# Fox q and k token-major, conditioning columns in another order and at other rates, five load buffers in turn

## The chip, the cores and the metric

The kernel runs on one core of a Trainium2 chip. The metric is the time of one execution in microseconds as the device reports it, the median of several runs. TensorE (PE) multiplies matrices, VectorE (DVE) and ScalarE (ACT) work on vectors, GpSimd (POOL) issues some of the transfers here and SyncE (SP) issues most of them. A weight load of PE is shown as PEld.

## What is computed

A trunk of two layers on 256 tokens of width 2048, all in float32. Both layers have the same frame; the mixer of the first is an mLSTM, that of the second is Forgetting Attention (Fox), and the change touches the second.

```
for layer in range(DEPTH):
    mod = cs @ ada_w[layer] + ada_b[layer]           # cs = silu(c); 6 vectors of 2048 a layer
    sh1, sc1, g1, sh2, sc2, g2 = split(mod, 6)
    h = rms_norm(x, norm_mix_w[layer]) * (1 + sc1) + sh1
    x = x + g1 * mixer(h)
    h = rms_norm(x, norm_ffn_w[layer]) * (1 + sc2) + sh2
    x = x + g2 * swiglu(h, ffn_w_gate_up[layer], ffn_w_down[layer])
return rms_norm(x, final_norm_w)

def fox_mixer(h, w_in, b_f, w_out):                  # 16 heads of 128
    q, k, v, fl = split(h @ w_in, [2048, 4096, 6144])
    cum = cumsum(log_sigmoid(fl + b_f))
    o = softmax(q @ k.T * 128 ** -0.5 + cum[t] - cum[s], causal) @ v
    return o @ w_out
```

The six vectors of `mod` are the conditioning columns: 2 layers of 96 columns of 128 values, each the product of a 128 x 2048 tile of `ada_w` with `cs`.

## The kernel before

**Matrix products.** A float32 weight is split into a high part `hi` (rounded to fp32r, on ACT, line 261) and a low part `lo` (the rest, on DVE, line 262); an activation is held the same way, 256 columns of high part and 256 of low part in one tile of 512. A product is the sum of high by high, high by low and low by high. There are two forms of it.

- Token-major (`group_a`, `mm_t`, lines 285 to 336): the activation's 128 tokens are the stationary operand, 512 weight columns stream. For each k tile of 128 and each of two token blocks there are three matmuls of 512 columns (lines 288, 289, 290). Two PSUM banks hold the result, tokens on partitions. All large products but one use it.
- Feature-major (`group_b`, `mm_b`, lines 269 to 308): the 128 weight columns are the stationary operand, the activation streams. For each k tile and each of four blocks of 128 features there is one matmul of 512 columns (`hi` with the high and the low half of the activation, line 271) and one of 256 (`lo` with the high half, line 274). Four banks hold the result, features on partitions; `total` (lines 366 to 374) adds the two halves. Only Fox's q and k use it, through the last two lines of `keep_t`, because the scores need features on partitions.

A column here is 512 output columns over all 16 k tiles; a tick follows every four k tiles. At a tick (`tick`, line 245) the kernel takes `adv` items from the list `steps`, which holds the work of attention heads and turned activations, and gives `n` credit to the background work `bg`, which issues one conditioning tile per whole credit.

**Loads.** `fetch` (line 250) loads 1 MB of weights on SP's queue, `ada_tile` (line 189) 1 MB of `ada_w`. Both take a buffer of the pool `rawp`, which has five under one tag; which of the five a load gets is settled by the framework's scheduler from those that it takes to be free. The same scheduler orders the instructions on each engine, except in the stretches under `manual_schedule`: the start, and the `bridge` between two parts of a layer.

**Conditioning.** `want(layer, vec)` queues 16 tiles. Ahead of the first FFN's second half these are queued: G2 of layer 0, SC1 and SH1 of layer 1, G1 of layer 1 (lines 1136 to 1138). At the start of Fox come SC2, SH2 and G2 of layer 1 (lines 1214, 1215). The rates are in `CFG`: `r0` for the four parts of the first FFN (gate and up, down, twice), `fr` for Fox, `r1` for the second FFN. A part that needs a vector that isn't done makes its tiles on the spot (`need`, line 227); a `Residual` needs its G.

**Turned activations of the FFN.** With `lag` (line 1158) the 256 x 512 product of gate and up is turned without PE: `blocks` transposes 32 x 32 blocks on DVE (line 353) and stores the result to DRAM from POOL's queue (line 357), `gather` reads it back with the blocks in place (line 361, four loads), and some ticks later `flip` splits it (lines 1171, 1172). As the transposes write it, four feature blocks lie side by side for each token: a block's tokens stand 4 elements apart.

**Fox.** `carry_on` and three v columns come first, then for each i of four one q column and one k column (lines 1293 to 1303), then `steps` gets the four heads of i, each with `scores` (line 1229 multiplies q and k), `flip` and `mix`. The fourth v column stands ahead of i = 2. What is left in `steps` is done at once ahead of the next heads (`drain`, line 1300), and after the last i ahead of k tile 12 of the first `fox_out` column (`project_out`, line 1097).

Of the kernel before, what the change touches and what calls it, by code (L numbers as in the profile page):

```python
# [17 lines left out]
P = 128  # L18
T = 256
# [6 lines left out]
QN = (6, 9)  # L26
CFG = dict(first=4, pace=(1.0, 1.0, 1.0), n2=4, lr=(0.9, 0.9, 0.95, 1.0, 1.15), sr=0.95, nsplit=11,
    r0=(0.75, 0.7, 0.8, 0.5), fr=0.66, r1=(0.3, 0.3, 0.3, 0.3))
# [3 lines left out]
def kernel(  # L32
# [9 lines left out]
    rawp = ctx.enter_context(tc.tile_pool(name="rawp", bufs=5))  # L42
# [145 lines left out]

    def ada_tile(layer, vec, k):
# [3 lines left out]
        nc.vector.scalar_tensor_tensor(  # L193
            out=raw, in0=raw, scalar=1.0, in1=cs, op0=ALU.mult, op1=ALU.mult,
            accum_out=acc[layer][:, j : j + 1],
        )
# [47 lines left out]

    def tick(n, adv=1):
        drain(adv)
        grow_all()
        bg(n)

    def fetch(w, k0, nk, c0):  # L250
        raw = rawp.tile([P, nk, 512], F32, tag="raw", name=nm("raw"))
        nc.sync.dma_start(raw, w[c0 // 512, k0 // 4, :, k0 % 4 : k0 % 4 + nk, :])
        return raw
# [15 lines left out]
    def mm_b(ps, hi, lo, rhs, first, last):  # L269
        def big():  # L270
            nc.tensor.matmul(ps, hi, rhs, start=first, stop=last, skip_group_check=True)  # L271

        def little():
            nc.tensor.matmul(  # L274
                ps[:, T:], lo, rhs[:, :T], start=False, stop=False, skip_group_check=True
            )

        if last:
            little()
            big()  # L280
        else:
            big()
            little()

# [10 lines left out]

    def group_b(w, nk, c0, act, evac, bgn, adv=1):
        banks = [bank() for _ in range(4)]
        for k in range(0, nk, 4):
            ws = load_w(w, k, 4, c0)
            for m in range(4):  # L300
                cols = slice(m * P, (m + 1) * P)
                for j, (hi, lo) in enumerate(ws):
                    mm_b(
                        banks[m], hi[:, cols], lo[:, cols], act(k + j), k + j == 0, k + j == nk - 1
                    )
                if k + 4 == nk:
                    evac(m, banks[m])
            tick(bgn, adv)
# [43 lines left out]
    def blocks(dst, src, aside):  # L352
        nc.vector.transpose(  # L353
            dst.rearrange("p (j b m) -> p j m b", j=4, m=4),
            src.rearrange("p (m j b) -> p j m b", m=4, j=4),
        )
        nc.gpsimd.dma_start(aside, dst)  # L357

    def gather(whole, aside):
        for j in range(4):  # L360
            nc.gpsimd.dma_start(
                whole[32 * j : 32 * j + 32].rearrange("a (g b) m -> a g (b m)", b=32),
# [3 lines left out]
    def total(ps, out, scale=None):  # L366
        b = t256()
        nc.scalar.activation(b, ps[:, T:], AF.Copy, scale=1.0 if scale is None else scale)
        if scale is None:
            nc.vector.tensor_tensor(out, ps[:, :T], b, op=ALU.add)  # L370
        else:
            nc.vector.scalar_tensor_tensor(
                out=out, in0=ps[:, :T], scalar=scale, in1=b, op0=ALU.mult, op1=ALU.add
            )
# [678 lines left out]

    def keep_t(c0, bgn, scale=None, adv=1, layer_w=0):
# [56 lines left out]
    def ffn(layer, begun, norm, rates, nsplit=0, srate=0.0, nxt=None):  # L1111
# [23 lines left out]
        if nsplit:  # L1135
            want(0, G2)
            want(1, SC1, SH1)
            want(1, G1)

# [8 lines left out]
        def swiglu(gr, lag):  # L1148
# [9 lines left out]
            if lag:  # L1158
                whole = slot().rearrange("p (t m) -> p t m", m=4)
# [5 lines left out]
            def flip(i):  # L1165
                acts[first + i] = dst = new_act()
                if lag:
                    ps = whole[:, :, 2 * i : 2 * i + 2].rearrange("p t m -> p m t")
                else:
                    ps = turned(sg, i)  # L1170
                nc.scalar.copy(dst[:, :, :T], ps)  # L1171
                nc.vector.tensor_tensor(  # L1172
                    dst[:, :, T:], ps, dst[:, :, :T].bitcast(F32), op=ALU.subtract
                )
# [39 lines left out]
    want(1, SC2, SH2)  # L1214
    want(1, G2)
# [5 lines left out]
    def fox_head(hd, q, k):  # L1221
        st = {}

        def scores():
            S = abank()
            logits(u3, hd, S, False)
            for t in range(2):
                n = P * (t + 1)
                nc.tensor.matmul(  # L1229
                    S[:, T * t : T * t + n], q[:, t * P : (t + 1) * P], k[:, :n],  # L1230
# [62 lines left out]
    for i in range(4):  # L1293
        if i == 1:
            vals[2] = keep_v(group_a(w, 2 * D + 1024, h_act, FR, ka=12, banks=begun[2 * D + 1024]))
# [127 lines left out]
```

## Time and profile before

| | |
|---|---|
| median of 3 runs | 2282.02 us (2279.6 to 2283.16) |
| profiled execution | 2279.4 us |
| its span, first to last instruction | 2277.6 us |
| mean granted TensorE clock | 0.999 |
| TensorE busy | 2255.0 us |
| VectorE busy | 1653.0 us |
| ScalarE busy | 1139.6 us |
| read from HBM | 628.44 MB, 281 GB/s read and written over the span |

A row of the groups of instructions names line, engine, operation, what is written and read, the shapes and the number; then come the busy time, the mean of one in ns, and the idle time of the engine ahead of them with what ended it. Matmuls overlap one another in the records, so their means are longer than their distance. A row of the chain of waits has start, length, and what ran. A row of the stretches has the stretch, its length, each engine's busy time with its number of instructions, the granted clock, the DMA engines' busy share and GB/s.

### The profile page before, as it was taken

Reading aid. Unit: us, or ns where it says so; the run is one execution under the profiler, and the core shown is the slowest. Engines: PE = TensorE matmul, PEld = TensorE weight load, DVE = VectorE, ACT = ScalarE, POOL = GpSimd, SP = SyncE. Lnnn points to the kernel's source line nnn. Section 1 sums busy time; section 2 is a strip of 40 time slices with the busy share of each in tenths; the row PEclk is TensorE's granted clock in tenths of the full one; section 3 lists DMA queues with packets and bytes.
Section 4 is the critical chain, followed back from the end, with each engine's and each line's share of the span. In section 5 each row is a group of like instructions: output and inputs, shape, how many; then the busy total and the mean of one; then the engine's idle time right before and its main releaser. Section 6 shows DMA issues by size and latency. Waiting matters only on the chain.

```text
span 2277.6 us, 26530 instructions
## 1 busy us (share of the span) xinstructions
PE 2255.0 (99%) x10250; PEld 1848.2 (81%) x10250; DVE 1653.0 (73%) x1865; ACT 1139.6 (50%) x1493; POOL 71.2 (3%) x136
## 2 busy tenths in 40 slices
PE   8999999999999999999999999999999999999998
PEld 5877878888888888888888888887888888888886
DVE  7998789878887878875687777777665555555564
ACT  4778564555543344444555444455444443444443
POOL 1000000000000000100000000000100100010000
PEclk9999999999999999999999999999999999999999
DMA  9998989788888889996667877675777665566662
GB/s 394 371 369 321 353 307 354 283 338 334 325 335 330 326 335 349 360 350 219 217 238 288 299 273 277 250 274 189 271 276 255 221 204 189 201 223 219 206 233 98
DMA packets 93571, 640.69 MB, mean 281 GB/s; under 512 B 11443, under 2 KB 11891, under 8 KB 19077
## 3 DMA queue, kind: packets, MB, share of 16 engines
q1 hardware_dynamic: 86400, 617.79, 73.5%
q0 software_dynamic: 6896, 21.08, 3.1%
q8 instruction: 80, 1.31, 0.2%
q14 instruction: 47, 0.38, 0.0%
q10 hardware_dynamic: 148, 0.14, 0.0%
HBM read 628.44 MB, written 10.52 MB: 281 GB/s over the span
## 4 chain that ended last, share of the span: by engine, by line
PE 87%; DVE 5%; DMA 4%; ACT 2%; issue 1%; POOL 0%; SPq 0%; ACTq 0%; DVEq 0%; POOLq 0%
PE mm L289 25%; PE mm L290 25%; PE mm L288 25%; PE mm L271 5%; PE mm L274 3%; DMA ada<-in_ada_w_dram 3%; DVE lo L262 2%; DVE ada L193 2%; ACT hi L261 1%; DMA slot<-in_w_in_dram 1%; PE aux L1010 0%; PE aux L498 0%; PE aux L1229 0%; PE mm L569 0%; PE mm L565 0%
## 5 line engine op out<-in xcount | busy, mean ns | idle before, releaser
L262 DVE TENSOR_TENSOR lo<-raw,hi 128x1024 fp32r<-128x1024 f32 x764 | 924.2, 1221 | 470.8 <-ACT hi L261 469.5
L261 ACT CAST hi<-raw 128x1024 fp32r<-128x1024 f32 x764 | 796.9, 1054 | 870.7 <-PE mm L290 742.2
L289 PE MATMUL mm<-lo,hT 128*128 128x512 f32 x1846 | 720.3, 390 | 3.3 <-DVE lo L262 3.2
L290 PE MATMUL mm<-hi,hT 128*128 128x512 f32 x1846 | 719.8, 390 | 0.0
L288 PE MATMUL mm<-hi,hT 128*128 128x512 f32 x1846 | 719.1, 392 | 0.0
L193 DVE SCALAR_TENSOR_TENSOR ada<-ada,cs 128x2048 f32<-128x2048 f32 x192 | 438.7, 2285 | 55.7 <-DMA ada<-in_ada_w_dram 55.3
L289 PEld LDWEIGHTS mm<-lo,hT 128*128 128x128 f32 x1846 | 346.7, 188 | 78.5 <-DVE lo L262 7.4
L290 PEld LDWEIGHTS mm<-hi,hT 128*128 128x128 f32 x1846 | 346.5, 188 | 72.4 <-issue 0.5
L288 PEld LDWEIGHTS mm<-hi,hT 128*128 128x128 f32 x1846 | 346.5, 188 | 71.9 <-issue 0.5
L288 PE MATMUL mm<-hi,slot 128*128 128x512 f32 x960 | 375.0, 391 | 0.2 <-ACT slot L1043 0.2
L289 PE MATMUL mm<-lo,slot 128*128 128x512 f32 x960 | 374.2, 390 | 0.2 <-DVE lo L262 0.2
L290 PE MATMUL mm<-hi,slot 128*128 128x512 f32 x960 | 374.1, 390 | 0.0
L288 PEld LDWEIGHTS mm<-hi,slot 128*128 128x128 f32 x960 | 180.3, 188 | 38.0 <-ACT slot L1043 0.8
L290 PEld LDWEIGHTS mm<-hi,slot 128*128 128x128 f32 x960 | 180.2, 188 | 37.7 <-issue 0.7
L289 PEld LDWEIGHTS mm<-lo,slot 128*128 128x128 f32 x960 | 180.2, 188 | 37.5 <-DVE lo L262 0.6
L271 PE MATMUL mm<-hT,hi 128*128 128x512 f32 x512 | 181.5, 401 | 0.0
L274 PE MATMUL mm<-hT,lo 128*128 128x256 f32 x512 | 138.4, 281 | 0.4 <-DVE lo L262 0.4
L271 PEld LDWEIGHTS mm<-hT,hi 128*128 128x128 f32 x512 | 94.4, 188 | 19.6
L274 PEld LDWEIGHTS mm<-hT,lo 128*128 128x128 f32 x512 | 96.6, 189 | 4.1 <-DVE lo L262 1.1
L865 ACT ACTIVATE slot<-mm 128x512 f32<-128x512 f32 x78 | 45.3, 596 | 39.7 <-PE mm L290 37.9
L357 POOL DMA_DIRECT2D aside<-t x32 | 18.0, 562 | 1239.7 <-DVE t L353 1239.7
L1172 DVE TENSOR_TENSOR slot<-slot,slot 128x512 fp32r<-128x512 f32 x32 | 34.8, 1090 | 24.8 <-ACT slot L1171 24.8
(220 smaller groups left out, 1049.6 us busy)
## 6 DMA issues: line engine op xcount, KB each, us to landing
ada<-in_ada_w_dram SPq DMA_DIRECT2D x192, 1024.0 KB, 6.3
raw<-in_gate_up_dram SPq DMA_DIRECT2D x176, 1024.0 KB, 5.2
raw<-in_down_dram SPq DMA_DIRECT2D x88, 1024.0 KB, 4.9
raw<-in_fox_in_dram SPq DMA_DIRECT2D x48, 1024.0 KB, 4.9
raw<-in_w_in_dram SPq DMA_DIRECT2D x44, 1024.0 KB, 7.2
raw<-in_w_out_dram SPq DMA_DIRECT2D x16, 1024.0 KB, 5.8
raw<-in_fox_out_dram SPq DMA_DIRECT2D x16, 1024.0 KB, 4.9
aside<-t POOLq DMA_DIRECT2D x32, 256.0 KB, 2.5
```

What stands on the lines that cost most here:

```text
L193: nc.vector.scalar_tensor_tensor(out=raw, in0=raw, scalar=1.0, in1=cs, op0=ALU.mult, op1=ALU.mult, accum_out=acc[layer][:, j : j + 1],)
L261: nc.scalar.copy(hi, raw[:, j : j + 2, :])
L262: nc.vector.tensor_tensor(lo, raw[:, j : j + 2, :], hi.bitcast(F32), op=ALU.subtract)
L271: nc.tensor.matmul(ps, hi, rhs, start=first, stop=last, skip_group_check=True)
L274: nc.tensor.matmul(ps[:, T:], lo, rhs[:, :T], start=False, stop=False, skip_group_check=True)
L288: nc.tensor.matmul(ps, a, hi, start=first, stop=False, skip_group_check=True)
L289: nc.tensor.matmul(ps, a, lo, start=False, stop=False, skip_group_check=True)
L290: nc.tensor.matmul(ps, b, hi, start=False, stop=last, skip_group_check=True)
L357: nc.gpsimd.dma_start(aside, dst)
L865: nc.scalar.activation(SP[i][:, t, :], banks[t], func)
L1172: nc.vector.tensor_tensor(dst[:, :, T:], ps, dst[:, :, :T].bitcast(F32), op=ALU.subtract)
```

## The change

- Fox q and k are computed token-major like the other columns and turned as the FFN's activations are. k stays as it was gathered; q is copied together by ACT six ticks after its k column (`LAND`; four for the last i), and a tick later its heads enter `steps`, two heads at a time. A new list `timed` in `tick` does this. `group_b`, `mm_b` and `total` go.
- `blocks` writes each feature block's tokens in runs of 32, which `gather`, `tiles` and `flip` follow, in the FFNs too.
- The fourth v column moves behind the last k column, and `project_out` of Fox computes the first twelve k tiles of two columns ahead of the last heads' end.
- SC2 and SH2 of layer 1 are queued ahead of G1, and G2 behind it, all in the first FFN; `r0` goes from (0.75, 0.7, 0.8, 0.5) to (0.75, 0.7, 0.65, 0.6) and `fr` from 0.66 to 0.52.
- `rawp` has five tags of one buffer each, and every load takes the next.

```diff
+RING = 5
 CFG = dict(first=4, pace=(1.0, 1.0, 1.0), n2=4, lr=(0.9, 0.9, 0.95, 1.0, 1.15), sr=0.95, nsplit=11,
-    r0=(0.75, 0.7, 0.8, 0.5), fr=0.66, r1=(0.3, 0.3, 0.3, 0.3))
+    r0=(0.75, 0.7, 0.65, 0.6), fr=0.52, r1=(0.3, 0.3, 0.3, 0.3))
...
-    rawp = ctx.enter_context(tc.tile_pool(name="rawp", bufs=5))
+    rawp = ctx.enter_context(tc.tile_pool(name="rawp", bufs=1))
...
+    def ring(name):
+        turn[0] += 1
+        return rawp.tile([P, D], F32, tag=f"raw{turn[0] % RING}", name=name)
...
-        raw = rawp.tile([P, D], F32, tag="raw", name=nm("ada"))
+        raw = ring(nm("ada"))
...
     def tick(n, adv=1):
+        clock[0] += 1
+        while timed and timed[0][0] <= clock[0]:
+            timed.pop(0)[1]()
         drain(adv)
...
     def fetch(w, k0, nk, c0):
-        raw = rawp.tile([P, nk, 512], F32, tag="raw", name=nm("raw"))
+        raw = ring(nm("raw"))[:, : nk * 512].rearrange("p (k c) -> p k c", c=512)
...
     def blocks(dst, src, aside):
         nc.vector.transpose(
-            dst.rearrange("p (j b m) -> p j m b", j=4, m=4),
+            dst.rearrange("p (j m b) -> p j m b", j=4, m=4),
             src.rearrange("p (m j b) -> p j m b", m=4, j=4),
         )
...
-                whole[32 * j : 32 * j + 32].rearrange("a (g b) m -> a g (b m)", b=32),
+                whole[32 * j : 32 * j + 32].rearrange("a (g c) -> a g c", c=P),
...
+    def tiles(whole):
+        return whole.rearrange("p (g m b) -> p m g b", m=4, b=32)
...
+    LAND = 6
...
-        o = slot().rearrange("p (k t) -> p k t", t=T)
-        group_b(w, KT, c0, h_act, lambda m, ps: total(ps, o[:, m, :], scale), bgn, adv)
-        return o
+        banks = group_a(w, c0, h_act, bgn, adv)
+        whole = slot()
+        aside = dram.tile([2, P, 512], F32, tag="aside", name=nm("aside"))
+        for t in range(2):
+            own = t512()
+            nc.scalar.activation(own, banks[t], AF.Copy, scale=1.0 if scale is None else scale)
+            blocks(t512(), own, aside[t])
+        gather(whole, aside)
+        return tiles(whole)
...
+        first = {}
+        if upto == 12:
+            for i in range(2):
+                first[i] = group_a(wo, 512 * i, act, bgn, adv, kb=upto, more=True)
+            assert not timed
+            drain()
         for i in range(3):
             res.both(i, group_a(
-                wo, 512 * i, act, bgn, adv, before=lambda k: drain() if k >= upto else None
+                wo, 512 * i, act, bgn, adv, ka=upto if i in first else 0, banks=first.get(i),
+                before=lambda k: drain() if k >= upto else None,
             ))
...
             want(1, SC1, SH1)
+            want(1, SC2, SH2)
             want(1, G1)
+            want(1, G2)
...
-    want(1, SC2, SH2)
-    want(1, G2)
...
-                    S[:, T * t : T * t + n], q[:, t * P : (t + 1) * P], k[:, :n],
+                    S[:, T * t : T * t + n].rearrange("p (g b) -> p g b", b=32),
+                    q[:, t * P : (t + 1) * P], k[:, : n // 32],
...
-        if i == 2:
-            vals[3] = keep_v(group_a(w, 2 * D + 1536, h_act, FR, 2))
-        q = keep_t(512 * i, FR, P ** -0.5, layer_w=1)
-        k = keep_t(D + 512 * i, FR, layer_w=1)
-        drain()
-        steps.extend(interleave(*[
-            fox_head(4 * i + j, q[:, j, :], k[:, j, :]) for j in range(4)
-        ]))
+        far = keep_t(512 * i, FR, P ** -0.5, 2, layer_w=1)
+        k = keep_t(D + 512 * i, FR, None, 2, layer_w=1)
+        q = slot().rearrange("p (m t) -> p m t", t=T)
+        heads = [fox_head(4 * i + j, q[:, j, :], k[:, j]) for j in range(4)]
+
+        def begin(q=q, far=far, heads=heads):
+            nc.scalar.copy(q.rearrange("p m (g b) -> p m g b", b=32), far)
+            timed.append((clock[0] + 1, lambda: steps.extend(
+                interleave(*heads[:2]) + interleave(*heads[2:])
+            )))
+
+        timed.append((clock[0] + (LAND if i < 3 else LAND - 2), begin))
+    vals[3] = keep_v(group_a(w, 2 * D + 1536, h_act, FR, 2))
```

More of the change, by code (lines that the diff above doesn't have):

```diff
@@ L187, in set_mods @@
         nc.vector.tensor_tensor(m, a, b, op=ALU.add)
+    turn = [0]
+    def ring(name):
+        turn[0] += 1
+        return rawp.tile([P, D], F32, tag=f"raw{turn[0] % RING}", name=name)
     def ada_tile(layer, vec, k):
         j = 16 * vec + k
-        raw = rawp.tile([P, D], F32, tag="raw", name=nm("ada"))
+        raw = ring(nm("ada"))
         nc.sync.dma_start(raw, ada_w[layer, j])
@@ L243, in drain @@
             steps.pop(0)()
+    clock = [0]
+    timed = []
     def tick(n, adv=1):
+        clock[0] += 1
+        while timed and timed[0][0] <= clock[0]:
+            timed.pop(0)[1]()
         drain(adv)
@@ L267, in load_w @@
         return [p for j in range(0, nk, 2) for p in split(raw, j)]
[L269 to L283, printed above, removed]
     def mm_t(ps, hi, lo, act, t, first, last):
@@ L294, in mm_a @@
             mm_t(ps[t], hi, lo, act, t, first, last)
[L296 to L308, printed above, removed]
     late = []
@@ L361, in gather @@
             nc.gpsimd.dma_start(
-                whole[32 * j : 32 * j + 32].rearrange("a (g b) m -> a g (b m)", b=32),
+                whole[32 * j : 32 * j + 32].rearrange("a (g c) -> a g c", c=P),
                 aside.rearrange("t (i a) c -> a (t i) c", a=32)[:, :, j * P : (j + 1) * P],
             )
[L366 to L374, printed above, removed]
+    def tiles(whole):
+        return whole.rearrange("p (g m b) -> p m g b", m=4, b=32)
     def split_act(src, dst):
@@ L1158, in swiglu @@
             if lag:
-                whole = slot().rearrange("p (t m) -> p t m", m=4)
+                whole = slot()
                 aside = dram.tile([2, P, 512], F32, tag="aside", name=nm("aside"))
@@ L1166, in flip @@
                 acts[first + i] = dst = new_act()
+                hi, lo = dst[:, :, :T], dst[:, :, T:]
                 if lag:
-                    ps = whole[:, :, 2 * i : 2 * i + 2].rearrange("p t m -> p m t")
+                    ps = tiles(whole)[:, 2 * i : 2 * i + 2]
+                    hi, lo = (x.rearrange("p m (g b) -> p m g b", b=32) for x in (hi, lo))
                 else:
                     ps = turned(sg, i)
[L1171 to L1174, printed above, removed]
+                nc.scalar.copy(hi, ps)
+                nc.vector.tensor_tensor(lo, ps, hi.bitcast(F32), op=ALU.subtract)
             steps.extend([lambda: None] * lag)
@@ L1294 @@
         if i == 1:
-            vals[2] = keep_v(group_a(w, 2 * D + 1024, h_act, FR, ka=12, banks=begun[2 * D + 1024]))
-        if i == 2:
-            vals[3] = keep_v(group_a(w, 2 * D + 1536, h_act, FR, 2))
-        q = keep_t(512 * i, FR, P ** -0.5, layer_w=1)
-        k = keep_t(D + 512 * i, FR, layer_w=1)
-        drain()
-        steps.extend(interleave(*[
-            fox_head(4 * i + j, q[:, j, :], k[:, j, :]) for j in range(4)
-        ]))
+            vals[2] = keep_v(
+                group_a(w, 2 * D + 1024, h_act, FR, 2, ka=12, banks=begun[2 * D + 1024])
+            )
+        far = keep_t(512 * i, FR, P ** -0.5, 2, layer_w=1)
[9 more added lines that the diff above has]
+    vals[3] = keep_v(group_a(w, 2 * D + 1536, h_act, FR, 2))
     res = Residual(1, G1, True)
```

## The prediction

> **What bounds the kernel now.** I read the busy shares first, then the chain that ended last, then the groups of instructions, and last the stretches of the span side by side.
>
> ```profile
> span 2277.6 us, 26530 instructions
> PE 2255.0 (99%) x10250; PEld 1848.2 (81%) x10250; DVE 1653.0 (73%) x1865; ACT 1139.6 (50%) x1493; POOL 71.2 (3%) x136
> ...
> PE 87%; DVE 5%; DMA 4%; ACT 2%; issue 1%; POOL 0%; SPq 0%; ACTq 0%; DVEq 0%; POOLq 0%
> ...
> L288 PE MATMUL mm<-hi,hT 128*128 128x512 f32 x1846 | 719.1, 392 | 0.0
> ...
> L271 PE MATMUL mm<-hT,hi 128*128 128x512 f32 x512 | 181.5, 401 | 0.0
> L274 PE MATMUL mm<-hT,lo 128*128 128x256 f32 x512 | 138.4, 281 | 0.4 <-DVE lo L262 0.4
> ```
>
> PE is idle for 2277.6 - 2255.0 = 22.6 us in all, and 87% of the chain is matmuls. So the time is the number of matmuls times the distance from one to the next, plus those 22.6 us. The mean of one (392, 401, 281 ns) is not that distance, because a matmul runs beside the next one. The distance is read from stretches in which PE never stops:
>
> ```profile
> 1850.00:2050.00 200.00, 200.00 (x884) 1.00 0.59 203
> ...
> 1225.00:1245.00 20.00, 20.00 (x115) 1.00 0.78 279
> 1355.00:1395.00 40.00, 40.00 (x229) 1.00 0.80 293
> ```
>
> The columns are the stretch, its length, PE's busy time with its matmuls, the granted clock, the DMA share and GB/s. In 1850:2050 PE runs only the three-matmul form of lines 288 to 290: 200 / 884 = 226 ns each. In the two lower stretches it runs only pairs of a 512-column and a 256-column matmul (lines 271, 274): 20 / 57.5 = 348 and 40 / 114.5 = 349 ns a pair. The clock is 1.00 throughout.
>
> **The change part by part.** *Fox q and k token-major.* The 512 pairs are 8 columns of 64 and are all removed: 512 x 0.349 = 178.7 us. In their place stand 8 columns of 16 x 2 x 3 = 96 matmuls: 768 x 0.226 = 173.6 us. **Gain 5.1 us**, all on PE and so on the path. Both forms stream as many columns a k tile (6 x 512 against 4 x 768 = 3072); what goes is the shorter matmul, whose pair takes 349 ns where 1.5 x 226 = 339 would do.
>
> The Trainium skill ("TensorE: Matmul & The Clock Gate", "Back-to-back issue gap") speaks against this gain: N / 2.4 + 2.5 ns a matmul gives 215.7 and 109.2 ns, so 4 pairs take 1299.6 and 6 long ones 1294.2 ns, which over 128 k tiles is an estimate of 0.7 us in place of 5.1. The trace disagrees with that rule: 226 where it says 215.7, 349 where it says 324.9.
>
> *What turns the columns.* Each column now needs two evacuations on ACT, two transposes on DVE, two stores and four loads on POOL's queue; each i one copy of q on ACT. Four ACT and four DVE half-width operations a column go.
>
> ```profile
> L865 ACT ACTIVATE slot<-mm 128x512 f32<-128x512 f32 x78 | 45.3, 596 | 39.7 <-PE mm L290 37.9
> L353 DVE STREAM_TRANSPOSE t<-slot 128x512 f32<-128x512 f32 x32 | 31.8, 1066 | 0.0
> L368 ACT ACTIVATE t<-mm 128x256 f32<-128x256 f32 x32 | 12.2, 383 | 17.5 <-PE mm L271 17.5
> L370 DVE TENSOR_TENSOR slot<-mm,t 128x256 f32<-128x256 f32 x16 | 6.5, 419 | 2.5 <-ACT t L368 2.5
> ...
> L361 POOL DMA_DIRECT2D slot<-aside x64 | 37.5, 592 | 64.9 <-DMA aside<-t 43.3 <-ACT hi L261 11.8 <-DMA raw<-in_gate_up_dram 5.8
> L357 POOL DMA_DIRECT2D aside<-t x32 | 18.0, 562 | 1239.7 <-DVE t L353 1239.7
> ```
>
> ACT: + 8 x 2 x 0.596 + 4 x 1.05 (a 128x1024 cast, line 261 below) - 12.2 = + 1.5 us. DVE: + 16 x 1.07 - 32 x 0.42 = + 3.7 us. POOL: 8 x (2 x 0.56 + 4 x 0.59) = 28 us on an engine that is 3% busy. All this lies beside the matmuls:
>
> ```profile
> 1350.00:1400.00 50.00, 50.00 (x287) 43.42 (x286) 35.20 (x42) 20.72 (x29) 0.00 (x0) 1.00 0.80 290
> 1444.00:1520.00 76.00, 76.00 (x355) 62.22 (x354) 55.29 (x77) 38.12 (x65) 0.00 (x0) 1.00 0.68 243
> ```
>
> (After the length come PE, PEld, DVE, ACT and POOL.) DVE has 14.8 us free in 50, ACT 29.3. The transfers add 0.5 MB out and 0.5 MB back a column (2 x 128 x 512 x 4 bytes), 8 MB or 35 GB/s over the 230 us of these columns, less the conditioning tiles that move away. I cost them at nothing; without that cover DVE's 3.7 us would be the price. The last heads before fox_out run in 1444:1520, where PE never stops, so spreading them over the first twelve k tiles of two columns costs and gains nothing. The last v column, with its four loads on SP's queue, moves behind the last k column unchanged in size; it fills the time that the last transposes need, and SP issues as many loads as before.
>
> *The waits that are new.* A copy of q waits on ACT for eight transfers, six ticks after its k column (four for the last i). Behind it on ACT stands the next cast to hi; behind that lo on DVE and then PE. A tick is 24 x 0.226 = 5.4 us. Transposed columns take this way already in the FFNs:
>
> ```profile
> L1171 ACT CAST slot<-slot x32: 1088/1123/1162, 884.6 to 2178.9; 128x512 fp32r<-128x512 f32 x32
> L1171 ACT CAST slot<-aux x12: 581/582/596, 568.4 to 690.1; 128x512 fp32r<-128x512 f32 x12
> ...
>   DMA slot<-aside: 19.9, 5
> ```
>
> ```profile
> 1814.54 4.05 DMA aside<-t
> ...
> 1822.32 7.91 DMA slot<-aside
> 1830.26 1.11 ACT slot L1171
> ```
>
> ```profile
> 1800.00:1850.00 50.00, 49.82 (x220) 40.91 (x219) 26.92 (x25) 20.71 (x20) 3.48 (x6) 1.00 0.65 214
> ```
>
> Of 32 casts 5 waited, 19.9 us together, and the late one at 1830.26 cost PE 0.18 us. From the second store to the landing took 1830.3 - 1814.5 = 15.7 us; with two evacuations and two transposes ahead of it, 2 x 0.6 + 2 x 1.07 = 3.3, that is 19 us from a column's end. Six ticks are 32.6 us, four 21.7. Bounds for four copies: 0 to 4 x 0.18 = 0.7; I take **0.6 us lost**, near the upper end, as the last i has only four ticks.
>
> *Runs of 32 tokens in the FFN.* The 32 casts of line 1171 read every fourth element and take 1123 ns, those from PSUM 582. If runs bring them to 582, ACT saves 32 x 0.54 = 17 us, and DVE's subtraction (line 1172) something alike. PE runs at its 226 ns there (1850:2050 above has such casts), so I count nothing, 0.2 us at most.
>
> *Conditioning and load buffers.* Busy time of the conditioning tiles' operation by stretch:
>
> ```profile
> 500.00:1000.00 500.00, 153.59 (x134) 1.00 0.91 339
> 1000.00:1100.00 100.00, 0.00 (x0) 1.00 0.69 235
> ...
> 1150.00:1500.00 350.00, 82.67 (x72) 1.00 0.74 271
> ```
>
> The queue runs dry at 1000:1100 and catches up in the Fox layer. The number of tiles stays; the new rates fill the hole. Worth something is only what PE loses now:
>
> ```profile
> 650.00:700.00 50.00, 49.31 (x227) 40.57 (x226) 38.84 (x40) 21.85 (x25) 1.58 (x3) 1.00 0.91 337
> ...
> 1500.00:1550.00 50.00, 48.42 (x219) 39.84 (x218) 33.17 (x42) 25.25 (x41) 0.00 (x0) 1.00 0.66 236
> ```
>
> ```profile
> 1530.05 1.24 DVE lo L262
> 1531.30 7.02 DMA ada<-in_ada_w_dram
> 1538.42 2.30 DVE ada L193 x2
> 1540.72 0.62 DVE t L442
> ```
>
> Idle: 0.69 + 1.58 = 2.3 us, the two largest losses between the first layer and the tail. The second is explained by the second fence: a buffer comes free at 1531.30, a conditioning tile's load starts into it, DVE waits for it, and the residual's operation stands behind it. With buffers in turn a tile's load goes out in the program's order, ahead of the bridge's weights, and fewer tiles are due there. I take **1.7 us gained** (1.4 of the 1.58, half of the 0.69); the ends are 0 and 2.3. What is late next is PE itself.
>
> **Sum:** - 5.1 + 0.6 - 1.7 = - 6.2 us. The profiled execution took 2279.4 us (span 2277.6 and 1.8 around it), 2.6 under the median of 2282.02; the gain is matmuls that every run has, so it is taken from both: 2273.2 for such an execution, **2275.8** for the median.
>
> **The rivals.** *The swap gains nothing.* If the 10 ns of a pair belong to what else the stage does and come back per column streamed, only the other terms stay: 2282.0 - 1.7 + 0.6 = 2280.9. Against it: the pair is 348 ns also in 1225:1245, where nothing stands between the pairs. This is also where the Trainium skill's gap formula, cited above, would land.
>
> *More stalls go.* The first layer loses PE time too:
>
> ```profile
> 100.00:150.00 50.00, 49.26 (x214) 39.59 (x213) 44.38 (x53) 37.14 (x57) 0.31 (x1) 1.00 0.99 364
> 150.00:200.00 50.00, 48.97 (x214) 39.76 (x214) 42.84 (x49) 36.95 (x57) 0.30 (x1) 1.00 0.95 356
> 200.00:250.00 50.00, 48.52 (x213) 39.21 (x212) 41.49 (x49) 37.00 (x54) 0.00 (x0) 1.00 0.88 339
> ```
>
> That is 0.74 + 1.03 + 1.48 = 3.3 us. If an even turn of buffers saves these and all of the 2.3: 2282.0 - 5.1 - 5.6 = 2271.3. Against it: DVE is 89% busy there and the DMA engines 99%; the order of buffers takes no work from either.
>
> *Strict turns hold back loads: slower.* In the same stretch a load that must wait for the one buffer whose turn it is, while another is free, comes late by one conditioning operation, and with DMA at 0.99 nothing makes that up.
>
> ```profile
> SPq L252 <- DVE ada L193: 322.4, 95, 9.0
> ...
> L193 DVE SCALAR_TENSOR_TENSOR ada<-ada,cs 128x2048 f32<-128x2048 f32 x192 | 438.7, 2285 | 55.7 <-DMA ada<-in_ada_w_dram 55.3
> L261 ACT CAST hi<-raw 128x1024 fp32r<-128x1024 f32 x764 | 796.9, 1054 | 870.7 <-PE mm L290 742.2 <-PE mm L271 42.9 <-issue 42.6
> ```
>
> Weight loads wait for a conditioning operation 95 times already. 100:250 holds some 27 k steps (643 matmuls / 24); one late by 2.285 us in every second: 13 x 2.3 = 30 us, of which I let half hide behind the two steps that wait split ahead of PE: about + 14, so 2275.8 + 14 = 2290. It decides from the point where buffers come free out of turn; DVE frees them in its own order, which speaks against it.
>
> *PE reads k in runs at half speed.* As ACT's cast (1123 against 582), the heads' score matmuls would double:
>
> ```profile
> 1267.18 0.66 PE aux L1229 x4
> ```
>
> 16 x 0.66 x 0.93 = + 9.8 us: 2285.6. Only one operand changes, and 32 elements stay together, not one. The Trainium skill ("SBUF — State Buffer", "Door 1: The DMA port swizzle") holds that consecutive accesses within a 16-byte line run at full bandwidth, so that runs of 32 would cost nothing and every fourth fp32 would; the casts agree with the second half, and no row of before shows the first.
>
> **How the numbers follow.** Forecast 0.56 (2273 to 2278.5); swap without gain 0.18; more stalls 0.14; strict turns 0.08; slow reads 0.04. A measurement tells 0.2%, 4.6 us, from no change. Faster by that (under 2277.4): the third case and most of the first, 0.65; slower (over 2286.6): strict turns, 0.08; the rest 0.27. The range 2269 to 2284 leaves out strict turns, half of the slow reads and a tail of the third case.
>
> **What would show it.** Right: no pairs, 768 more matmuls on lines 288 to 290 at 226 ns, the Fox columns some 5 us shorter, 1500:1550 idle under 0.5, casts of line 1171 near 600 ns. Wrong: PE idle in the Fox layer behind ACT's copies; 100:250 with fewer matmuls than 214 in 50 us; score matmuls above 0.66 us a head.

## The result

| | before | after |
|---|---|---|
| median | 2279.60 us (2276.99 to 2283.16, 7 runs) | 2290.75 us (2285.53 to 2300.91, 7 runs) |
| profiled execution | 2279.4 us | 2291.9 us |
| its span | 2277.6 us | 2290.1 us |
| mean granted clock | 0.999 | 0.996 |
| TensorE busy | 2255.0 us | 2254.4 us |
| TensorE idle (span less busy) | 22.6 us | 35.7 us |

The ratio is 1.0054, with a 95% interval of 1.0032 to 1.0076: the change is slower by about half a per cent, where 0.3% less was forecast.

The page of the profile after, its heads and the operation of the conditioning tiles:

```profile
span 2290.1 us, 26059 instructions
...
PE 2254.4 (98%) x9994; PEld 1839.9 (80%) x9994; DVE 1628.7 (71%) x1849; ACT 1127.5 (49%) x1481; POOL 99.0 (4%) x184
...
PE 83%; DMA 7%; DVE 6%; issue 2%; ACT 2%; SPq 0%; ACTq 0%; DVEq 0%
...
L200 DVE SCALAR_TENSOR_TENSOR ada<-ada,cs 128x2048 f32<-128x2048 f32 x192 | 438.9, 2286 | 96.2 <-DMA ada<-in_ada_w_dram 95.9
```

There are 256 fewer matmuls, as the swap of 512 pairs for 768 long ones must leave, but PE is hardly less busy. Its share of the chain falls by 4 points and that of the DMA rises by 3. DVE's wait ahead of a conditioning operation goes from 55.3 us to 95.9 us over the same 192 tiles. So the engine that now waits more is DVE, and for the conditioning tiles.

Where PE lost it, by stretches of the span, before (the columns are those of the prediction, with all five engines):

```profile
650.00:1180.00 530.00, 528.92 (x2353) 436.44 (x2352) 403.71 (x413) 237.57 (x265) 22.70 (x39) 1.00 0.83 306
1180.00:1500.00 320.00, 319.56 (x1707) 270.54 (x1706) 243.08 (x338) 154.25 (x257) 0.00 (x0) 1.00 0.76 278
```

and after:

```profile
650.00:1180.00 530.00, 527.57 (x2342) 435.91 (x2341) 409.35 (x428) 231.35 (x263) 21.13 (x36) 1.00 0.85 317
1180.00:1500.00 320.00, 307.19 (x1401) 251.11 (x1400) 218.53 (x294) 151.58 (x237) 29.41 (x51) 0.98 0.78 276
```

In the Fox layer (1180:1500) PE's idle time rises from 0.44 to 12.81 us, and the granted clock there is 0.98. The first FFN (650:1180) loses 1.35 us more, the bridge behind Fox gains 1.58 (1500:1550, shown further down). So 12.4 of the 13.1 us by which PE's idle time grew lie in the layer whose q and k were rewritten.

What happens there, in the chain of waits around the largest loss (start, length, what ran):

```profile
1299.88 2.29 DVE lo L275 x2
...
1302.18 10.73 DMA ada<-in_ada_w_dram
...
1312.93 0.04 DVE ada L200
...
1315.15 0.08 DVE ada L200
1315.23 0.08 DVE r L1240
...
1316.35 0.29 DVE slot L1243
...
1316.77 0.45 PE aux L934
```

and the same moment in the timeline of DVE (start, length, line, operation, then in brackets how long the engine had been idle and for what):

```profile
1306.86 0.41 DVE L1231 TENSOR_REDUCE den<-aux 128x1 f32<-128x256 f32 x1
1312.93 2.29 DVE L200 SCALAR_TENSOR_TENSOR ada<-ada,cs 128x2048 f32<-128x2048 f32 x1 [5.65 <-DMA ada<-in_ada_w_dram]
```

and of PE:

```profile
1309.20 0.49 PE L934 MATMUL aux<-ident,slot 128*128 128x128 f32 x3
1316.77 0.45 PE L934 MATMUL aux<-ident,slot 128*128 128x128 f32 x1 [7.09 <-DVE slot L1243]
```

Read upwards from the last row. PE stands 7.09 us at a transpose of a head's softmax weights, because DVE has not scaled them (line 1243). DVE has not, because the conditioning operation stands ahead of the reciprocal (line 1240) and the scaling in its queue, and that one waits for its tile. The tile's load began at 1302.18, right when line 275 freed its buffer, and took 10.73 us to land. Nothing ran on DVE from 1307.27 to 1312.93: everything behind the tile waited 5.65 us for the landing and then 2.29 us for the operation, and a `lo` of 1.2 us ran ahead of the scaling besides. Over the whole layer PE stood three times at such a transpose, 11.7 us in all, and once for `lo`, 1.1 us; that is the 12.81. The second longest stop, 3.52 us at 1432.86, has the same chain, behind a tile that took 8.75 us.

The same tile in Fox over all its loads (idle time of DVE with its number of times, and the time from issue to landing), before:

```profile
  DMA ada<-in_ada_w_dram: 24.5, 20
...
DMA to landing us min/median/max: 4.6/4.9/6.6
```

and after:

```profile
  DMA ada<-in_ada_w_dram: 44.8, 21
...
DMA to landing us min/median/max: 4.7/6.3/10.7
```

DVE waited for a tile about as many times before. Each wait was 1.2 us and stayed hidden from PE; after, it is 2.1 us, and the longest reach PE. The landing has grown, and the new traffic in this layer is the scratch that the turned q and k columns write to DRAM and read back from POOL's queue. That is the theory with which the experiments began: **the scratch transfers delay conditioning tiles, and DVE, waiting for one in order, holds up the heads' softmax and `lo`.** Rivals were the strict turn of the five buffers, the new rates and order of the conditioning columns, and the two heads that now run at a time.

### The profile page after: what moved, and what is told of

It reads as the page before. It is cut to its first block, busy times and chain, and to the rows that moved or that the text cites. A ratio compares the mean times of both kernels' runs of the same rounds, so it can differ in the third digit from the quotient of the medians.

```text
span 2290.1 us, 26059 instructions
## 1 busy us (share of the span) xinstructions
PE 2254.4 (98%) x9994; PEld 1839.9 (80%) x9994; DVE 1628.7 (71%) x1849; ACT 1127.5 (49%) x1481; POOL 99.0 (4%) x184
## 4 chain that ended last, share of the span: by engine, by line
PE 83%; DMA 7%; DVE 6%; issue 2%; ACT 2%; SPq 0%; ACTq 0%; DVEq 0%
PE mm L287 26%; PE mm L286 26%; PE mm L285 26%; DMA ada<-in_ada_w_dram 6%; DVE lo L275 3%; DVE ada L200 2%; DMA slot<-in_w_in_dram 1%; ACT hi L274 1%; PE aux L474 0%; PE mm L545 0%; PE mm L541 0%; PE mm L542 0%; PE aux L329 0%; PE aux L986 0%; PE aux L934 0%
## 5 line engine op out<-in xcount | busy, mean ns | idle before, releaser
L286 PE MATMUL mm<-lo,hT 128*128 128x512 f32 x2102 | 821.9, 391 | 4.3 <-DVE lo L275 4.3
L285 PE MATMUL mm<-hi,hT 128*128 128x512 f32 x2102 | 821.8, 393 | 0.0
L287 PE MATMUL mm<-hi,hT 128*128 128x512 f32 x2102 | 821.3, 391 | 0.0
L200 DVE SCALAR_TENSOR_TENSOR ada<-ada,cs 128x2048 f32<-128x2048 f32 x192 | 438.9, 2286 | 96.2 <-DMA ada<-in_ada_w_dram 95.9
L286 PEld LDWEIGHTS mm<-lo,hT 128*128 128x128 f32 x2102 | 395.7, 188 | 89.3 <-DVE lo L275 8.1
L287 PEld LDWEIGHTS mm<-hi,hT 128*128 128x128 f32 x2102 | 395.5, 188 | 82.6 <-issue 0.5
L285 PEld LDWEIGHTS mm<-hi,hT 128*128 128x128 f32 x2102 | 395.8, 188 | 81.4 <-issue 0.5
L286 PEld LDWEIGHTS mm<-lo,slot 128*128 128x128 f32 x960 | 180.7, 188 | 39.8 <-DVE lo L275 2.7
L340 POOL DMA_DIRECT2D aside<-t x48 | 27.0, 563 | 1155.5 <-DVE t L336 1057.9
L841 ACT ACTIVATE slot<-mm 128x512 f32<-128x512 f32 x78 | 45.2, 596 | 39.8 <-PE mm L287 38.1
L344 POOL DMA_DIRECT2D slot<-aside x96 | 56.2, 592 | 133.7 <-DMA aside<-t 84.7
L424 ACT ACTIVATE t<-X 128x512 f32<-128x512 f32 x32 | 20.1, 630 | 45.1 <-DVE X L419 43.3
L1167 DVE TENSOR_TENSOR slot<-slot,slot 128x512 fp32r<-128x512 f32 x32 | 22.0, 687 | 18.7 <-ACT slot L1166 18.7
L1145 ACT ACTIVATE slot<-mm 128x512 f32<-128x512 f32 x44 | 25.6, 598 | 15.0 <-PE mm L287 14.8
L419 DVE TENSOR_TENSOR X<-X,t 128x512 f32<-128x512 f32 x48 | 32.3, 686 | 0.5
```

Of the source, the lines that this page charges most:

```text
L200: nc.vector.scalar_tensor_tensor(out=raw, in0=raw, scalar=1.0, in1=cs, op0=ALU.mult, op1=ALU.mult, accum_out=acc[layer][:, j : j + 1],)
L285: nc.tensor.matmul(ps, a, hi, start=first, stop=False, skip_group_check=True)
L286: nc.tensor.matmul(ps, a, lo, start=False, stop=False, skip_group_check=True)
L287: nc.tensor.matmul(ps, b, hi, start=False, stop=last, skip_group_check=True)
L344: nc.gpsimd.dma_start(whole[32 * j : 32 * j + 32].rearrange("a (g c) -> a g c", c=P), aside.rearrange("t (i a) c -> a (t i) c", a=32)[:, : ...
L419: nc.vector.tensor_tensor(cols, cols, m, op=ALU.add)
```

## The experiments

Each ran beside the kernel before on the same chip (2280.59 us beside e1 to e4, 2279.42 beside e5 to e8, 2280.08 beside e9 to e11). Idle times are PE's, span less busy, in the one profiled execution of each.

| run | median us (range, runs) | ratio, 95% interval | PE idle: span | 650:1180 | 1180:1500 |
|---|---|---|---|---|---|
| before, after | 2279.60, 2290.75 | 1.0054 (1.0032 to 1.0076) | 22.6, 35.7 | 1.08, 2.43 | 0.44, 12.81 |
| e1_pool | 2304.04 (2297.31 to 2306.28, 5) | 1.0097 (1.0082 to 1.0112) | 37.7 | 7.51 | 11.58 |
| e2_rates | 2286.80 (2284.28 to 2288.69, 8) | 1.0025 (1.0015 to 1.0035) | 31.7 | 4.85 | 8.41 |
| e3_noload | 2273.94 (2272.43 to 2275.21, 6) | 0.9972 (0.9961 to 0.9983) | 22.2 | 0.70 | 0.47 |
| e4_turn | 2284.28 (2278.49 to 2285.97, 12) | 1.0016 (1.0007 to 1.0024) | 25.2 | 3.39 | 1.53 |
| e5_moved | 2283.05 (2281.94 to 2285.24, 11) | 1.0014 (1.0005 to 1.0023) | 28.8 | 7.40 | 0.00 |
| e6_feature | 2280.18 (2276.32 to 2283.36, 11) | 0.9997 (0.9988 to 1.0006) | 23.2 | 4.35 | 0.33 |
| e7_nowait | 2276.83 (2273.61 to 2283.29, 11) | 0.9989 (0.9980 to 0.9999) | 24.3 | 3.21 | 1.86 |
| e8_later | 2278.68 (2275.12 to 2280.53, 11) | 0.9992 (0.9983 to 1.0001) | 25.9 | 0.41 | 0.00 |
| e9_apart | 2269.79 (2269.17 to 2272.70, 5) | 0.9959 (0.9946 to 0.9971) | 21.1 | 2.40 | 0.00 |
| e10_noswap | 2277.17 (2275.05 to 2280.37, 11) | 0.9988 (0.9979 to 0.9997) | 19.5 | 1.44 | 0.00 |
| e11_poolapart | 2269.47 (2268.24 to 2274.03, 5) | 0.9956 (0.9943 to 0.9968) | 18.2 | 0.27 | 0.00 |

### The turn of the buffers undone

```diff
-    rawp = ctx.enter_context(tc.tile_pool(name="rawp", bufs=1))
+    rawp = ctx.enter_context(tc.tile_pool(name="rawp", bufs=5))
...
-        return rawp.tile([P, D], F32, tag=f"raw{turn[0] % RING}", name=name)
+        return rawp.tile([P, D], F32, tag="raw", name=name)
```

> The changed kernel with the five load buffers as one pool again, all else as changed. Late tiles (the new scratch transfers of q and k lengthen the conditioning tiles' loads, DVE stands in order before a tile that has not landed, and lo and the softmax stand behind it): nothing of that is undone, so DVE's wait for tiles in 1200:1500 stays over 30 us (44 in the changed kernel), PE's idle time over the span stays 30 to 40 us (35.7 there, 22.6 before), 2284 to 2296 us. Strict turns (a load waits for one certain buffer): PE's idle time falls to 20 to 25 us and the time to 2272 to 2278 us.

Not faster but slower still, by 13 us of medians; 2304.04 us lies above both ranges that were expected, while DVE's wait for tiles in Fox (42.9 us in 1180:1500) and PE's idle time are as the first of them had it. Its stretch of the first FFN:

```profile
650.00:1180.00 530.00, 522.49 (x2308) 429.86 (x2308) 402.98 (x422) 226.89 (x256) 21.13 (x36) 0.99 0.85 312
```

PE loses 7.51 us there, 5 more than after, and Fox still loses 11.58 us, so the strict turn is not what costs; by this run it rather helps, above all in the first FFN. Why the free choice is worse there was not followed up; e11_poolapart, below, takes the point away.

### The conditioning's order and rates undone

```diff
-    r0=(0.75, 0.7, 0.65, 0.6), fr=0.52, r1=(0.3, 0.3, 0.3, 0.3))
+    r0=(0.75, 0.7, 0.8, 0.5), fr=0.66, r1=(0.3, 0.3, 0.3, 0.3))
...
-            want(1, SC2, SH2)
             want(1, G1)
-            want(1, G2)
...
+    want(1, SC2, SH2)
+    want(1, G2)
```

> The changed kernel with the conditioning order and rates of before (SC2, SH2 and G2 queued at the start of Fox, r0 and fr as before). Late tiles: some 36 tiles in 1150:1500 in place of 28, each of which can come late, so PE's idle time 35 to 50 us and 2290 to 2305 us. New rates as the cause: PE's idle time 20 to 25 us, 2272 to 2278 us. If the spread is worth what it was forecast (1.7 us) and late tiles do not depend on their number: 2291 to 2294 us.

A greater loss was expected in Fox, and that was a miss: Fox loses 8.41 us in place of 12.81, although a tile now takes 7.7 us to land in the median and 11.9 at most. DVE waited 21.2 us in 9 times, not 44.8 in 21. So the slow landing alone doesn't set the loss; what fits is how often DVE comes to a tile before it has landed, which the rates shift. The number of tiles was hardly put to the test: 29 in 1180:1500 against 27. Of the 4.85 us lost in 650:1180, 4.42 lie in 1150:1180, at the bridge into Fox. The time, 2286.80 us, lies in none of the three ranges, and the interval of its ratio overlaps that of the change, so it isn't shown that the new rates cost anything by themselves.

### No conditioning loads in Fox

```diff
-        nc.sync.dma_start(raw, ada_w[layer, j])
+        if not dry[0]:
+            nc.sync.dma_start(raw, ada_w[layer, j])
...
-            out=raw, in0=raw, scalar=1.0, in1=cs, op0=ALU.mult, op1=ALU.mult,
+            out=raw, in0=cs if dry[0] else raw, scalar=1.0, in1=cs, op0=ALU.mult, op1=ALU.mult,
...
+    dry[0] = True
...
+    dry[0] = False
```

`dry` holds from Fox's first column to the start of `fox_out`.

> The changed kernel, but the conditioning tiles made between the start of Fox and the last attention head are not loaded: the same DVE operation reads cs in place of the tile. This leaves out those columns of the conditioning. Late tiles: DVE has nothing to wait for there, PE's idle time falls to 18 to 24 us and the time to 2270 to 2277 us. Strict turns: the tiles still take their turns and weight loads still wait for their buffers, so PE's idle time stays over 28 us and the time over 2283 us. Heads two at a time (PE reaches the transposes of the weights before DVE and ACT have made them, whatever is loaded): the gaps at these transposes stay, over 28 us idle, over 2283 us.

Fox in the stretches of this run:

```profile
1180.00:1500.00 320.00, 319.53 (x1479) 262.53 (x1478) 233.81 (x312) 161.00 (x250) 29.54 (x51) 1.00 0.64 222
```

The loss is gone, 0.47 against 12.81 us, with heads two at a time, copies of q, scratch and DVE's operation all in place. What cost was the conditioning tiles' loads or the wait for them. This run also removes 1 MB a tile of traffic, so it doesn't say which of the two.

### q and k turned on PE, without the scratch

```diff
-        whole = slot()
-        aside = dram.tile([2, P, 512], F32, tag="aside", name=nm("aside"))
+        sg = pair(slot())
+        o = slot().rearrange("p (m t) -> p m t", t=T)
         for t in range(2):
-            own = t512()
-            nc.scalar.activation(own, banks[t], AF.Copy, scale=1.0 if scale is None else scale)
-            blocks(t512(), own, aside[t])
-        gather(whole, aside)
-        return tiles(whole)
+            nc.scalar.activation(sg[:, t, :], banks[t], AF.Copy, scale=1.0 if scale is None else scale)
...
+            nc.scalar.copy(o[:, 2 * i : 2 * i + 2, :], turned(sg, i))
```

> The changed kernel, but Fox's q and k columns are turned on PE (16 transposes a column, 128 at 0.11 us: 14 us more on PE) in place of DVE and the scratch in DRAM; conditioning and turns as changed. Late tiles, with the scratch transfers as what makes them late: tiles land in 4.9 us median in 1200:1500 again (6.3 in the changed kernel), PE's idle time 20 to 25 us, so 2290.1 - 12 - 4 (clock back at 1.00) + 14 = 2286 to 2291 us of span. Heads two at a time or strict turns: PE's idle time stays over 30 us and the time comes to 2300 us or more.

The conditioning tile in Fox, in this run:

```profile
  DMA ada<-in_ada_w_dram: 16.2, 12
...
DMA to landing us min/median/max: 4.7/5.0/7.5
```

Without the scratch a tile lands as fast as it did before (4.9 and 6.6 there), DVE waits 16.2 us instead of 44.8, and PE's loss in Fox is 1.53 us. With e6_feature, which has no scratch in Fox either and the same 5.0 us in the median, this shows that the scratch lengthens the landing. (e9_apart and e10_noswap, below, differ by the scratch too, with 27 loads each in 1180:1500: 6.0 us in the median and 9.6 at most with it, 4.9 and 6.3 without.) The time stays above that of before because turning on PE costs PE itself: 2257.0 us busy with 10058 matmuls, against 2249.3 with 9994 in e9_apart. That is 64 transposes and 7.7 us, part of it half clock behind a stop of 3.10 us at 1059.15; the expectation counted 128 and 14 us, and so the span, 2282.2 us, came out under its range.

### The same tiles taken out of Fox's q and k

```diff
-    r0=(0.75, 0.7, 0.65, 0.6), fr=0.52, r1=(0.3, 0.3, 0.3, 0.3))
+    r0=(0.9, 0.88, 0.77, 0.8), fr=0.52, r1=(0.45, 0.3, 0.3, 0.3))
...
-    FR = CFG["fr"]
+    FR = 1.0
...
+    FR = 0.0
...
+    FR = CFG["fr"]
```

The rate is 1.0 for the first columns of Fox, 0 for its q and k columns, and as in the change from `fox_out` on.

> The changed kernel, but no conditioning tile is issued in Fox's q and k stretch: r0 (0.9, 0.88, 0.77, 0.8), the rate of Fox 1.0 up to the first q column, 0 in the four q and k pairs, 0.52 in fox_out, 0.45 in the first part of the second FFN. Nothing is left out. Late tiles: PE's idle time in 1180:1500 falls from 12.8 to under 2 us and the time to 2273 to 2278 us, if the denser tiles of the first FFN cost at most 3 us of PE there (650:1180 lost 2.4 in the changed kernel); if they cost more, the loss shows in 650:1180 and the time is 2279 to 2286. Heads two at a time or turns as the cause: 1180:1500 keeps 8 us or more.

Half a success. Its stretches:

```profile
650.00:1180.00 530.00, 522.60 (x2299) 427.15 (x2298) 435.44 (x456) 221.91 (x249) 19.55 (x33) 1.00 0.90 343
1180.00:1500.00 320.00, 320.00 (x1484) 263.39 (x1484) 198.14 (x272) 162.93 (x255) 29.37 (x51) 1.00 0.69 236
```

In Fox PE no longer stops at all. The tiles went into the first FFN, where they bring the DMA engines to 0.90 busy, and there PE loses 7.40 us. That is another loss than the one in Fox: in 650:1180 DVE waits for no tile, but ACT waits 39.8 us for weights to cast, where it waited 2.2 us in the change and 11.4 in before. So there was no free place to move them to at these rates.

### All of the change but the swap

This is before with the ring of buffers, the runs of 32 tokens in the FFN and the new order and rates; q and k stay in pairs, feature-major. What came with the swap is as in before too: the heads' start, the place of the fourth v column, and `project_out`. The lines that make q and k, against after:

```diff
-        banks = group_a(w, c0, h_act, bgn, adv)
...
-        gather(whole, aside)
-        return tiles(whole)
+        o = slot().rearrange("p (k t) -> p k t", t=T)
+        group_b(w, KT, c0, h_act, lambda m, ps: total(ps, o[:, m, :], scale), bgn, adv)
+        return o
```

> The kernel before with everything of the change but Fox's q and k: buffers in turn, runs of 32 in the FFN's turned activations, new conditioning order and rates. Late tiles: without scratch transfers in Fox the tiles land in 5 us there, PE idle in 1180:1500 under 1.5 us, 2277 to 2281 us (the forecast's 1.7 us gained, less what 1000:1100 loses). If turns or rates made the loss by themselves: 2284 us or more.

```profile
1180.00:1500.00 320.00, 319.67 (x1707) 270.19 (x1706) 228.24 (x321) 154.95 (x259) 1.64 (x3) 1.00 0.71 260
```

The ratio is 0.9997: these parts together are worth nothing that can be measured. In its profile they lose 4.35 us in the first FFN, where before lost 1.08, and save in the bridge. In Fox PE loses 0.33 us: the loss there comes with the swap and what belongs to it.

### Loaded, but not waited for

```diff
-            out=raw, in0=raw, scalar=1.0, in1=cs, op0=ALU.mult, op1=ALU.mult,
+            out=slot().bitcast(BF16) if dry[0] else raw, in0=cs if dry[0] else raw, scalar=1.0, in1=cs, op0=ALU.mult, op1=ALU.mult,
```

> The changed kernel, but in Fox a conditioning tile is loaded and not read: DVE's operation reads cs and writes a bf16 scratch in place of the load's buffer. This leaves out those columns of the conditioning; the loads and their traffic stay. If DVE's waiting in front of a tile is what costs: PE idle in 1180:1500 under 2 us and 2272 to 2278 us, as without the loads (2273.9). If the traffic itself delays weights or turned columns: idle stays over 6 us there and the time over 2281 us.

```profile
1180.00:1500.00 320.00, 318.14 (x1468) 260.54 (x1467) 230.08 (x308) 159.67 (x247) 29.40 (x51) 1.00 0.81 288
```

All loads of the change are there, the DMA share is even 0.81 for 0.78, and a tile takes 7.1 us in the median to land. Yet PE loses 1.86 us in place of 12.81. This tells e3_noload's two readings apart: the traffic as such costs little, the wait for it costs the rest. One thing more differs here: no operation of DVE holds the load's buffer. e9_apart, below, reads every tile again and holds its buffer longer, and settles that.

### The operation a tick later

If the wait is the cause, nothing has to be taken away: the tile's load can go out where it does, and DVE's operation a tick later, behind `lo`.

```diff
-            ada_tile(layer, v, k)
+            waiting.append((layer, v, k, ada_tile(layer, v, k)))
...
+    def catch_up():
+        while waiting:
+            layer, v, k, raw = waiting.pop(0)
+            with tc.issue_after(last_lo[0].ins):
+                ada_use(layer, v, k, raw)
...
     def tick(n, adv=1):
...
+        catch_up()
         grow_all()
         bg(n)
```

> The changed kernel, but each background tile's DVE operation is queued one tick later, behind the next tick's last lo on DVE, while its load is issued at the same place. Nothing is left out. If DVE's place for the tile is too near the load's landing: waits for tiles fall by half or more (44.8 us in 1180:1500), PE idle there from 12.8 to under 5 us, 2274 to 2282 us. If loads go out late because buffers are held: a tile held a tick longer makes it worse, over 2291 us.

Right in Fox, and not ahead of it:

```profile
250.00:650.00 400.00, 395.73 (x1792) 319.22 (x1791) 328.58 (x388) 221.23 (x318) 1.90 (x4) 1.00 0.83 317
```

In Fox DVE waits for no tile any more and PE never stops, and the first FFN loses 0.41 us. But 250:650 now loses 4.27 us, where after loses 1.22, and 0:250 loses 12.40 for 10.48. A tile's buffer is held a tick longer; in 250:650 PE now waits 3.4 us for `lo` and 0.6 for `hi`. That buffers are the reason there is argued, not shown.

### A tick later from the first FFN on, and two counterparts

e9_apart is the same edit with a switch that is set ahead of the first FFN. e10_noswap puts that edit on e6_feature. e11_poolapart is e9_apart with the free pool of five.

```diff
+            if apart[0]:
+                with tc.issue_after(last_lo[0].ins):
+                    ada_use(layer, v, k, raw)
+            else:
+                ada_use(layer, v, k, raw)
...
+    apart[0] = True
```

> The changed kernel with a background tile's DVE operation a tick behind its load from the first FFN on, and at once in the first layer's mixer as before. Nothing is left out. Late tiles, and a place on DVE a tick later as the cure: PE idle under 1 us in 1180:1500 and in 650:1180, as in e8_later (0.00 and 0.41), and 1.0 to 1.5 us in 250:650 (4.3 there), so 2278.7 less 5 to 7 us: 2271 to 2275 us, faster than both kernels. If e8_later's gain in Fox was owed to something in the first layer: 2277 us or more.

> As e9_apart, but Fox's q and k in pairs on PE as before the change (e6_feature with the tiles' operations a tick later). It differs from e9_apart in the swap alone, and neither should stall in Fox. If the pair's 10 ns are real: 5.1 us over e9_apart by the forecast's sum, 4 to 8 us over it measured, 2276 to 2281 us. If the swap gains nothing on PE: within 2 us of e9_apart.

> As e9_apart, but with the five load buffers as one pool. If turns matter by themselves (with the pool the changed kernel lost 7.5 us of PE in 650:1180, with turns 2.4): 3 us idle or more in 650:1180 and 2276 to 2285 us. If they matter only by the order in which tiles come due on DVE, and that is settled by the later place: within 2 us of e9_apart.

The page and, in a second view, the stretch of Fox of e9_apart:

```profile
PE 2249.3 (99%) x9994; PEld 1836.4 (81%) x9994; DVE 1632.3 (72%) x1849; ACT 1126.2 (50%) x1481; POOL 99.3 (4%) x184
```

```profile
1180.00:1500.00 320.00, 320.00 (x1481) 263.04 (x1480) 233.40 (x311) 162.09 (x252) 29.51 (x51) 1.00 0.84 291
```

and its conditioning tiles there, for which DVE has no wait left:

```profile
DMA to landing us min/median/max: 4.7/6.0/9.6
```

The tiles still take up to 9.6 us to land, with the scratch beside them at a DMA share of 0.84, and neither DVE nor PE waits for them. **2269.79 us is 21 us under after and beats both kernels**, by a ratio of 0.9959 to before. It needs no other rates and no fewer bytes. The time is even under the 2271 to 2275 us that were expected; the first FFN is not, it loses 2.40 us where under 1 was. e11_poolapart has the same time, 2269.47: with the wait gone, the turn of the buffers is worth nothing either way.

e10_noswap is e9_apart without the swap. Its page:

```profile
PE 2255.4 (99%) x10250; PEld 1849.6 (81%) x10250; DVE 1632.1 (72%) x1865; ACT 1122.6 (49%) x1493; POOL 71.4 (3%) x136
```

The swap, with the scratch, the heads' start, the v column's place and the `project_out` that came with it, is 2277.17 - 2269.79 = 7.4 us by the medians, and 2255.4 - 2249.3 = 6.1 us of PE's busy time. The intervals of the two ratios don't overlap; the ratios differ by 0.0029 or 6.6 us, and their intervals leave room for some 3 to 10. Without the swap the later place brings little: 0.9988 to before (0.9979 to 0.9997), where e6_feature, beside other runs of before, had 0.9997.

## Why the prediction was wrong

**The account.** The profiled span grew by 12.5 us: 13.1 more of idle PE, less 0.6 of busy PE. The 0.6 is what the swap saves, 2255.0 - 2249.3 = 5.7 us of before against e9_apart, less 2254.4 - 2249.3 = 5.1 us that the same 9994 matmuls took longer in after than in e9_apart. They took longer because some ran at half clock: the clock falls after the long stops. Right behind the stop shown above, with a granted clock of 0.55:

```profile
1317.00:1322.00 5.00, 5.00 (x15) 3.96 (x15) 1.02 (x1) 0.48 (x1) 0.00 (x0) 0.55 0.97 377
```

That is 1.6 us more than 15 x 0.226. Each of the three stops of over 2 us behind the first layer (2.29, 7.09 and 3.52 us) is followed by some eight to ten matmuls 0.43 us apart instead of 0.23, which comes to some 5 us together.

**The swap: right, its size as near as can be told.** 5.1 us were forecast; 6.1 were measured by busy time, 7.4 by medians, and the ratios leave room for the 5.1. The 226 ns holds after, 884 matmuls in 200 us:

```profile
1850.00:2050.00 200.00, 200.00 (x884) 165.68 (x883) 105.78 (x100) 80.18 (x80) 6.66 (x12) 1.00 0.58 204
...
1500.00:1550.00 50.00, 50.00 (x225) 41.47 (x224) 36.47 (x40) 28.07 (x41) 0.00 (x0) 1.00 0.73 267
650.00:700.00 50.00, 50.00 (x230) 41.30 (x229) 42.24 (x43) 21.31 (x25) 1.58 (x3) 1.00 0.87 340
100.00:150.00 50.00, 49.28 (x215) 39.87 (x214) 44.38 (x53) 37.15 (x58) 0.30 (x1) 1.00 0.97 363
```

Whether the 1 to 2 us between are real was not found. The first rival, that the swap gains nothing, fell, and with it the 0.7 us that the gap formula of the Trainium skill gave. The Trainium skill ("TensorE: Matmul & The Clock Gate", "Back-to-back issue gap") gives that formula for an isolated matmul, and this kernel is a stream of weight loads and matmuls.

**What turns the columns: the step that failed.** The prediction put it so: "All this lies beside the matmuls", and of the transfers "I cost them at nothing". As work they do lie beside them, and a transpose of q or k took 0.71 us where 1.07 was put. But with them the landing of the conditioning tiles went from 4.9 to 6.3 us in the median and from 6.6 to 10.7 at most, and DVE waits for those in order. The landing alone is not the cost: in the first FFN of before a tile took 7.2 us in the median and 12.2 at most, and PE lost 1.08 us there. The row that should have warned was quoted: DVE was idle 55.3 us ahead of conditioning operations. I read it as slack of an engine with 14.8 us free in 50. It was a wait that happened to end before anyone needed what stood behind it, and the change lengthened it. The check to make was not whether DVE has time, but what stands behind the waiting instruction in its queue: the softmax scaling that PE's transposes need, and `lo`.

**The copies of q: no loss, where 0.6 was put.** They and the turned FFN casts, by line (number; least, median and greatest ns; first and last start):

```profile
L1296 ACT COPY slot<-slot x4: 1043/1048/1050, 1294.8 to 1452.0; 128x1024 f32<-128x1024 f32 x4
```

```profile
L1166 ACT CAST slot<-slot x32: 611/619/632, 884.5 to 2190.2; 128x512 fp32r<-128x512 f32 x32
```

No copy waited for the transfers, so six ticks and four were enough; the new wait that the prediction looked at was on the wrong engine.

**Runs of 32 tokens: as forecast.** The casts fell from 1123 to 619 ns, near the 600 that was named, off the path, and e6_feature shows no gain of it.

**Conditioning and buffers: right in place, not seen in the sum.** 1500:1550 and 650:700, in the fence above, are at no loss, as forecast or better. But a new one has come in the first FFN:

```profile
1045.14 9.84 DMA ada<-in_ada_w_dram
...
1055.07 2.30 DVE ada L200 x2
1057.37 1.15 DVE lo L275
...
1058.56 0.72 PE mm L286
```

It is the same mechanism: a tile that takes 9.84 us, `lo` behind it, PE behind `lo`. The 1.7 us don't show: in e6_feature PE is idle 23.2 us where it was 22.6 in before, though its ratio of 0.9997 (0.9988 to 1.0006) is too coarse to tell 1.7 us from nothing. Filling the hole at 1000:1100 brought tiles and their waits into it; in e2_rates, with the old rates, PE doesn't stop in 1000:1100.

**The other rivals.** More stalls go: not in the first layer, 215 matmuls in 100:150 against 214. Strict turns: slower was right, and even the 2290 us that this rival gave, but by luck, since e1_pool is slower without turns and e11_poolapart the same. (Its sum has two slips that change nothing: the rows give 641 matmuls, not 643, and half of 30 us is 15, not 14.) Slow reads of k: four score matmuls take 0.67 us for 0.66 (in the chain of waits after), so runs of 32 cost PE nothing. That agrees with what the prediction cited of the 16-byte lines in the Trainium skill ("SBUF — State Buffer", "Door 1: The DMA port swizzle"), as do the casts:

```profile
1332.11 0.67 PE aux L1220 x4
```

**What stays open.** The order in which the scheduler puts DVE's instructions can be read only from when they ran; that a tile's operation stands just where its landing is due is inferred from such moments, and e7_nowait and e9_apart agree with it. Why e1_pool is so much worse than after, and what PE loses in the first FFN of e9_apart (2.40 us, and 0.27 in e11_poolapart, one profile each), was not settled.

## What to carry to other kernels

An engine that works in order and waits for a load is not idle: list what stands behind the waiting instruction, and whether the change makes that load land later, before calling its time free. New transfers, even on another queue, are to be costed as later landing of the loads that somebody waits for. The cure was to issue the consumer one step later than the load, behind the work that others need, and not everywhere: in the first layer the same edit cost PE 3 us in 250:650 (4.27 for 1.22).

## What was not expected of the hardware

The half clock comes after shorter stops than I had thought. PE's timeline after, around the stop at 1055.88:

```profile
1055.88 0.39 PE L285 MATMUL mm<-hi,slot 128*128 128x512 f32 x1
1058.56 0.72 PE L286 MATMUL mm<-lo,slot 128*128 128x512 f32 x1 [2.29 <-DVE lo L275]
1059.08 0.63 PE L287 MATMUL mm<-hi,slot 128*128 128x512 f32 x1
1059.51 0.63 PE L285 MATMUL mm<-hi,slot 128*128 128x512 f32 x1
...
1062.79 0.39 PE L285 MATMUL mm<-hi,slot 128*128 128x512 f32 x1
1063.02 0.39 PE L286 MATMUL mm<-lo,slot 128*128 128x512 f32 x1
```

After 2.29 us without work the matmuls start 0.43 us apart, not 0.23, for about 3.5 us. The Trainium skill ("TensorE: Matmul & The Clock Gate", "What's actually happening") has the clock halved after at least one idle window of about 3.4 us. Here the trace differs: 2.29 us was enough, and the measurement decides. It is no threshold, though: in e1_pool a stop of 2.59 us ahead of 1402.19 is followed by matmuls 0.23 us apart, and behind the stop of 3.52 us in after the first 1.3 us of matmuls ran so before the clock fell. What decides was not found. The second surprise is how much 256 KB stores and their gathers, on a queue of their own and at a DMA share of 0.78, lengthen 1 MB loads on SP's queue: 6.3 us in the median for 4.9, and at most 10.7 for 6.6.
